# Latent attention rows in a two-layer diffusion backbone: the softmax division on GpSimd, and a fixed order of the small steps

## The chip, the cores and the metric

The kernel runs on one core of a Trainium2 chip. The metric is the device time of one execution in microseconds (us), taken as the median of repeated runs. TensorE does the matmuls and transposes, VectorE and ScalarE the elementwise work out of PSUM, GpSimd (POOL in the profile) elementwise work between SBUF tiles, and SyncE issues most of the loads.

## The reference, cut to what matters

Two layers of a diffusion backbone, on 512 latent tokens and 256 context tokens, float32 throughout. Layer 0 mixes by two head groups side by side: four heads of gated linear attention (GLA) and eight heads of softmax attention. The change lies in layer 0, where the latent queries attend to all 768 keys while the readouts of the GLA heads (second pair) are finished:

```python
def _softmax_attend(q, k, v):
    s = jnp.einsum('bhgqd,bhkd->bhgqk', q, k, preferred_element_type=jnp.float32) * (ATT_HEAD_DIM ** -0.5)
    p = jax.nn.softmax(s, axis=-1).astype(v.dtype)
    return jnp.einsum('bhgqk,bhkd->bhgqd', p, v)

def _gated_readout(o, og, gain):
    return _merge(_rms(o, gain) * jax.nn.silu(og))
```

The results of both groups stand side by side (`cat`), and one output projection follows, then the feed-forward parts and layer 1.

## The kernel before, in words

**The stage.** `Attention.latent` (L285 on) works through 32 rows, one for each of four tiles of 128 latent tokens and each of eight heads; a row is a 128x768 block of probabilities. It is a generator with 37 steps: step i makes the scores of row i, turns row j = i - 3, and in every second step multiplies two turned rows with the values. The steps of one row:

- `scores` (L178): four matmuls of TensorE into an `S` tile (tag `mm`, two buffers of two banks each); VectorE takes the row minimum (`amx`, L193; the scores carry a minus sign), ScalarE the exponential with its sum (`prob`, `asm`, L195), VectorE the reciprocal of the sum (`ars`, L196) and the division, as a multiplication by a per-partition scalar (L198).
- `turned` (L200): three steps later six transposes `pT`, the first four into a `tr` tile (two buffers), the last two into one of the two single banks `sc0` and `sc1`; then two copies back to SBUF (`probT`, L210), 128x512 and 128x256. ScalarE does both, except that VectorE takes the second one in every fourth row.
- `values` (L212): 24 matmuls into `attO`, which takes the `sc` bank of its token tile (t % 2). After the last head of a tile, `done` (L231) has ScalarE round the result to `x` (L763) and VectorE form the remainder (L764).
- `other` (L148) says which `sc` bank the transposes may use: the one that `attO` does not hold, or, once a tile is in the list `ended`, that tile's own bank. `done` puts the tile on the list at once, so that the next step's transposes go to the bank that L763 and L764 are just reading.
- `queries` (L166), after steps 4, 12 and 20: four transposes `qT` (in a `tr` tile), then ScalarE, VectorE, ScalarE, VectorE take one half each (`qs`, L174 and L175).

**The work behind it.** The table `behind` in `even_mixer` (L1270) names what follows the attention step i: `t` transposes a readout (`catT`, L1329 on) and splits it into `x` (L1330, L1331); `r1` is one readout of the second head pair (L1222 on) for two token tiles; `M` is a group of modulation columns: 64 small matmuls `mod_acc`, and later `modT`. A readout takes squares on ScalarE (`sq`, L1228), their sum on VectorE (L1230), a power on GpSimd (`rs`, L686), and two VectorE multiplications of 128x512 elements with both inputs in SBUF, by `rs` (L1233) and by the gate `og` (L1235).

**What sets the order.** TensorE's instructions keep the order in which the program is written (`pin`). On VectorE, ScalarE and GpSimd a scheduler chooses the order from the dependencies, and it may pull a step ahead of its place in the program: of the three `r1`, two run before row 0 of the latent attention, and one in the middle of the loop. The splits of weights for the output projection (`wH` on ScalarE, L803; `wL<-raw,wH` on VectorE, L804, both inputs in SBUF) are placed by the scheduler as well. A pair of existing functions fixes an order: `order_from` (L1594) remembers the last instruction written, and `order_to` makes each later instruction of an engine depend on the one written before it on that engine.

Of the kernel before, what the change touches and what calls it, by code (L numbers as in the profile page):

```python
# [8 lines left out]
F32 = mybir.dt.float32  # L9
# [3 lines left out]
AF = mybir.ActivationFunctionType  # L13
ALU = mybir.AluOpType
AX = mybir.AxisListType
PSUM = bass.MemoryType.PSUM

P = 128
# [4 lines left out]
NT = SEQ + CTX  # L23
NTT = NT // P
LT = SEQ // P
# [108 lines left out]
class Attention:  # L134
# [150 lines left out]
    def latent(self, ap):  # L285
        kl = [ap.tile([P, 2, SEQ], F32R, name=f"k{x}") for x in "HL"]
        self.k[0] = [kl] + self.k[1]
        q = lambda t: ap.tile([P, 8, P], F32R, tag="qs", bufs=2, name=f"qs{t}")
        self.keys(0, LT, kl)
        yield  # L290
        self.queries(0, q(0))
        yield

        ahead = 3
        ps, pTs, due = {}, {}, []
        for i in range(8 * LT + ahead + 2):
            t, hd = divmod(i, 8)
            if t < LT:
                ps[i] = ap.tile([P, NT], F32, tag="prob", bufs=4, name="prob")
                self.scores(t, (hd,), ps[i][:, None, :])  # L300
            j = i - ahead
            if 0 <= j < 8 * LT:
                pTs[j] = ap.tile([P, NTT, P], F32, tag="probT", bufs=4, name="probT")
                self.turned(ps.pop(j), pTs[j], (1,) if j % 4 == 3 else (), self.other())
            if due:
                t0, n, xs = due.pop()
                self.values(t0, n, xs)
                if n == 3:
                    self.done(t0)
            if 0 <= j < 8 * LT and j % 2:  # L310
                due.append((j // 8, j // 2 % 4, [pTs.pop(x) for x in (j - 1, j)]))
            if t + 1 < LT and hd == 4:
                self.queries(t + 1, q(t + 1))
            yield


class Net:
# [797 lines left out]
    def even_mixer(self, h, mix, z):  # L1115
        nc, I = self.nc, self.I
# [5 lines left out]
        tiles = (4, 0, 2)  # L1122
# [84 lines left out]
        def job(c, i):  # L1207
            t0, nt = ((LT, 2), (0, LT))[i]
            ends.setdefault(c, [])
            return self.gla_job(gp, c, t0, nt, fs[c][i], gq[c], gk[c], gv, *((ends[c], None) if i else (None, ends[c])))  # L1210
# [11 lines left out]
        def readout(c, tiles=tiles):  # L1222

            for t0 in tiles:
                cs = slice(256 * c, 256 * c + 256)
                o = gv[:, t0 : t0 + 2, cs].rearrange("p t (h v) -> p t h v", h=2)
                sq = self.wp.tile([P, WU], F32, tag="mraw", bufs=2, name="sq")[:, :512]
                nc.scalar.activation(sq.rearrange("p (t n) -> p t n", t=2), gv[:, t0 : t0 + 2, cs], AF.Square)  # L1228
                ss = self.sm.tile([P, 4], F32, tag="ss4", name="ss4")
                nc.vector.tensor_reduce(ss, sq.rearrange("p (x v) -> p x v", v=P), axis=AX.X, op=ALU.add)  # L1230
                rs = self.rstd(ss, P, 4)
                rb = rs.rearrange("p (t h) -> p t h", t=2)[:, :, :, None].to_broadcast([P, 2, 2, P])
                nc.vector.tensor_tensor(o, o, rb, op=ALU.mult)  # L1233
                x = gv[:, t0 : t0 + 2, cs]
                nc.vector.scalar_tensor_tensor(x, x, 0.5 if c else 1.0, og[c][:, t0 : t0 + 2, :], op0=ALU.mult, op1=ALU.mult)  # L1235


        kinds = {
            "q": lambda: nat(1536 + 288, ev_q), "kv": lambda: nat(1536 + 544, ev_kv), "m": lambda: mods,
            "qk0": lambda: qk(0), "qk1": lambda: qk(1), "v0": lambda: values(0), "v1": lambda: values(1),  # L1240
            "g0": lambda: gates(0), "g1": lambda: gates(1), "p": lambda: self.att_prep(mixg, natq, natk),
            "c0": lambda: job(0, 0), "l0": lambda: job(0, 1), "c1": lambda: job(1, 0), "l1": lambda: job(1, 1),
            "e": decays, "r0": lambda: (readout(0, (t,)) for t in tiles), "r1": lambda: (readout(1, (t,)) for t in tiles),
            "x": lambda: att.context(), "y": lambda: att.latent(ap),
            "t": lambda: self.gated_T(lambda t, hh: gv[:, t, hh * P : (hh + 1) * P], 4, R_GG, cat, ((4, 2), (0, 4))),
            "M": lambda: self.mod_group(0, 4, ["wL"] * 4 + ["wH"] * 3 + ["raw"]),
# [2 lines left out]
        att = Attention(self, natq, natk, cat)  # L1249
        running = {"qk0": early}  # L1250

        def run(steps):
            for x in steps.split():
                if x not in running:
                    running[x] = kinds[x]()
                next(running[x], None)
# [10 lines left out]
        with self.pool("att") as ap:  # L1267
            run("y x y g1 x y x y M x y")

            behind = {6: "t", 7: "r1", 9: "t", 10: "r1", 14: "M", 15: "r1", 16: "M", 17: "t", 19: "t", 22: "t", 24: "t", 26: "t", 29: "t"}  # L1270
            for i in range(3, 32 + 5):
                run("y " + behind.get(i, ""))
        self.pinned = False
        return cat

# [1009 lines left out]
```

## Time and profile before

| | |
|---|---|
| median of 3 runs | 1674.96 us (1674.84 to 1675.24) |
| the profiled execution | 1675.78 us, its span 1674.0 us |
| TensorE (PE) busy | 1644.8 us, 98% of the span |
| VectorE (DVE) busy | 1311.1 us, 78% |
| ScalarE (ACT) busy | 916.1 us, 55% |
| GpSimd (POOL) busy | 129.4 us, 8% |
| granted TensorE clock | 0.998 of full speed |

The span is what the profiler sees of the program; 1.8 us of the execution's time lie around it. The profiled execution is a run of its own, 0.8 us longer than the median. In the page, "L198" is line 198 of the kernel, `out<-in` are the program's names of the tiles, and "idle before" is how long the engine stood still ahead of those instructions, with the engine that ended the wait behind an arrow. A span of a group in a timeline is pipelined: the next instruction may start before the shown end of the one in front of it.

### The profile page before, as it was taken

What the parts mean: (1) busy time and instruction counts of PE and PEld (TensorE: products, weight loads), DVE (VectorE), ACT (ScalarE), POOL (GpSimd) and SP (SyncE); (2) the same over time, 40 slices, a digit from 0 to 9 for tenths busy, and PEclk for the clock granted to TensorE, in tenths of its full rate; (3) what the DMA queues carried; (4) which work ended last, traced back from release to release, by engine and by line L of the source; (5) the groups of instructions that cost most, each with busy time, mean ns of one, the idle gap of its engine ahead of it and who ended that gap; (6) DMA issues with size and microseconds to landing.
All of it is one profiled execution on the core that took longest, in us unless ns stands there. A gap on an engine that the chain in (4) does not pass through costs nothing.

```text
span 1674.0 us, 32524 instructions
## 1 busy us (share of the span) xinstructions
PE 1644.8 (98%) x13407; PEld 1481.1 (88%) x13407; DVE 1311.1 (78%) x2097; ACT 916.1 (55%) x1551; POOL 129.4 (8%) x139
## 2 busy tenths in 40 slices
PE   9999999999999999999999999999999999999998
PEld 7899987888999999998887888888888899999886
DVE  5999678976898988777668648788775599987887
ACT  5745567845544443446447436666664565555664
POOL 2004110011000000002102000000000100000310
PEclk9999999999999999999999999999999999999999
DMA  9641012164243445249525541121124333333973
GB/s 336 213 132 41 3 45 86 50 227 160 80 126 114 139 151 176 78 153 205 100 84 193 200 127 57 48 65 40 51 65 150 126 114 115 114 101 102 226 164 138
DMA packets 184736, 204.79 MB, mean 122 GB/s; under 512 B 7142, under 2 KB 141836, under 8 KB 184588
## 3 DMA queue, kind: packets, MB, share of 16 engines
q1 hardware_dynamic: 173996, 181.98, 34.7%
q0 software_dynamic: 9024, 17.30, 5.9%
q10 hardware_dynamic: 1568, 3.43, 0.6%
q8 instruction: 105, 1.72, 0.4%
q14 instruction: 43, 0.35, 0.1%
HBM read 193.23 MB, written 9.46 MB: 121 GB/s over the span
## 4 chain that ended last, share of the span: by engine, by line
PE 83%; DVE 8%; ACT 3%; DMA 3%; issue 2%; POOL 0%; SPq 0%; DVEq 0%; ACTq 0%; POOLq 0%
PE nat L355 12%; PE a L355 10%; PE ff L355 8%; PE E L355 7%; PE oproj L355 6%; PE x L355 6%; PE o L355 5%; PE D L355 4%; PE b L355 3%; PE fq L355 3%; PE gqk L355 2%; PE pearly L355 2%; PE q L355 2%; PE S L355 2%; PE poh L355 1%
## 5 line engine op out<-in xcount | busy, mean ns | idle before, releaser
L355 PE MATMUL nat<-wH,x 128*128 128x256 f32 (+2 forms) x968 | 226.7, 322 | 1.2 <-ACT x L2014 0.6
L860 ACT CAST wH<-raw 128x1024 fp32r<-128x1024 f32 x120 | 124.8, 1051 | 102.7 <-DVE raw L885 40.7
L355 PEld LDWEIGHTS nat<-wH,x 128*128 128x128 f32 x968 | 161.9, 190 | 19.5 <-ACT natq L1196 1.7
L861 DVE TENSOR_TENSOR wL<-raw,wH 128x1024 fp32r<-128x1024 f32 x120 | 145.7, 1222 | 23.6 <-ACT wH L860 23.3
L355 PE MATMUL nat<-wL,x 128*128 128x256 f32 (+2 forms) x484 | 153.5, 317 | 1.8 <-DVE wL L804 1.8
L804 DVE TENSOR_TENSOR wL<-raw,wH 128x1024 fp32r<-128x1024 f32 x79 | 95.8, 1222 | 50.6 <-ACT wH L803 49.8
L355 PE MATMUL ff<-x,wH 128*128 128x512 f32 (+1 forms) x512 | 127.6, 340 | 0.0
L686 POOL TENSOR_TENSOR rs<-ms,neghalf 128x1 f32<-128x1 f32 (+2 forms) x56 | 60.1, 1076 | 777.7 <-DVE ms L684 777.6
L803 ACT CAST wH<-raw 128x1024 fp32r<-128x1024 f32 x79 | 82.2, 1050 | 68.5 <-PE ff L355 19.7
L355 PE MATMUL oproj<-wH,x 128*128 128x512 f32 x320 | 102.2, 394 | 0.4 <-ACT x L1330 0.4
L355 PEld LDWEIGHTS nat<-wL,x 128*128 128x128 f32 x484 | 92.1, 190 | 7.8 <-DVE wL L804 2.7
L615 DVE SCALAR_TENSOR_TENSOR macc<-mraw,scT,macc 128x1024 f32<-128x1024 f32 x70 | 88.0, 1282 | 11.6 <-DMA mraw<-in_mod_w_dram 11.4
L355 PEld LDWEIGHTS ff<-x,wH 128*128 128x128 f32 x512 | 87.3, 190 | 10.0
L355 PE MATMUL x<-wH,two 128*128 128x512 f32 x280 | 90.5, 392 | 0.9 <-DVE y L1851 0.7
L1773 POOL DMA_DIRECT2D t<-in_ffn_w_down_dram x36 | 41.9, 1200 | 640.1 <-DVE t L1812 338.3
L1012 ACT COPY qkh<-arr 128x512 f32<-128x512 f32 x112 | 70.2, 641 | 36.6 <-DVE arr L1017 32.3
L355 PE MATMUL ff<-x,wL 128*128 128x256 f32 (+1 forms) x256 | 86.2, 337 | 0.0
L885 DVE TENSOR_TENSOR raw<-raw 128x512 f32<-128x512 f32 x120 | 82.8, 690 | 2.8
L1017 DVE TENSOR_TENSOR arr<-arr,f 128x512 f32<-128x512 f32 x112 | 74.4, 688 | 2.0 <-ACT qkh L1012 0.3
L355 PEld LDWEIGHTS oproj<-wH,x 128*128 128x128 f32 x320 | 59.9, 188 | 13.0 <-ACT x L1330 1.0
L355 PE MATMUL a<-T,wH 128*128 128x384 f32 (+1 forms) x320 | 70.5, 309 | 0.6 <-ACT qb L923 0.5
L355 PE MATMUL E<-T,wH 128*128 128x384 f32 (+1 forms) x320 | 70.4, 309 | 0.7 <-DVE go L938 0.7
(425 smaller groups left out, 4558.6 us busy)
## 6 DMA issues: line engine op xcount, KB each, us to landing
mraw<-in_mod_w_dram SPq DMA_DIRECT2D x80, 512.0 KB, 4.4
raw<-in_ffn_w_gate_dram SPq DMA_DIRECT2D x44, 512.0 KB, 3.9
raw<-in_ffn_w_up_dram SPq DMA_DIRECT2D x44, 512.0 KB, 4.9
raw<-in_odd_w_in_dram SPq DMA_DIRECT2D x40, 512.0 KB, 3.7
t<-in_ffn_w_down_dram POOLq DMA_DIRECT2D x30, 512.0 KB, 8.3
raw<-in_ffn_w_down_dram SPq DMA_DIRECT2D x28, 512.0 KB, 8.0
mraw<-in_mod_w_dram SPq DMA_DIRECT2D x32, 256.0 KB, 6.3
raw<-in_even_w_in_dram SPq DMA_DIRECT2D x16, 512.0 KB, 5.9
```

The source lines that it names most:

```text
L355: return self.pin(self.nc.tensor.matmul(*a, **k))
L615: nc.vector.scalar_tensor_tensor(a, u, w, a, op0=ALU.mult, op1=ALU.add)
L686: nc.gpsimd.tensor_tensor(rs, ms, self.neghalf.to_broadcast([P, w]), op=ALU.pow)
L803: self.casts = self.casts[-1:] + [nc.scalar.copy(H[:, :m], raw[:, :m])]
L804: vector.tensor_tensor(L[:, :m], raw[:, :m], H[:, :m].bitcast(F32), op=ALU.subtract)
L860: self.nc.scalar.copy(H, f)
L861: self.nc.vector.tensor_tensor(L, f, H.bitcast(F32), op=ALU.subtract)
L885: add = lambda o, x, y: nc.vector.tensor_tensor(o, x, y, op=ALU.add)
L1012: nc.scalar.copy(qkv[:, :, :, half, :], dst)
L1017: nc.vector.tensor_tensor(dst, dst, tb, op=ALU.mult)
L1773: add = lambda o, src: self.pin(nc.gpsimd.dma_start(out=o, in_=src, accum_op=ALU.add))
```

## The change

1. The division of a latent row moves from VectorE to GpSimd: a `tensor_tensor` multiplication of the 128x768 row by the reciprocal, broadcast along the row. It is written at step i for row i - 1, together with the reciprocal. The rows (`prob`) get six buffers in place of four.
2. The copies after the transposes are divided by a rule: the 128x512 one always on ScalarE, the 128x256 one always on VectorE.
3. Within a step the order is now written as: scores (TensorE); reciprocal and division of row i - 1; minimum of row i; transposes of row j; ScalarE's copy; exponential of row i; VectorE's copy; values. `order_from` and `order_to` around the loop keep ScalarE, VectorE and GpSimd to this order from step 3 on.
4. A finished tile's bank is put on the list `ended` one step later (`over`).
5. A readout of the second pair becomes a generator of four pieces (squares; sum and power; multiplication by `rs`; multiplication by `og`), and `behind` places the twelve pieces of the three readouts one by one between steps 3 and 16. The modulation group moves from steps 14 and 16 to 17 and 22, and the `t` pieces from 6 to 29 to between 8 and 28.

```diff
@@ Attention.latent
-        ps, pTs, due = {}, {}, []
+        ps, pTs, sums, due, over = {}, {}, {}, [], []
         for i in range(8 * LT + ahead + 2):
             t, hd = divmod(i, 8)
             if t < LT:
-                ps[i] = ap.tile([P, NT], F32, tag="prob", bufs=4, name="prob")
-                self.scores(t, (hd,), ps[i][:, None, :])
+                s = net.mm_tile("S")
...
+            if i - 1 in sums:
+                p, sm = ps[i - 1], sums.pop(i - 1)
+                r = net.sm.tile([P, 1], F32, tag="ars", name="ars")
+                nc.vector.reciprocal(r, sm)
+                self.scaled = nc.gpsimd.tensor_tensor(p, p, r.to_broadcast([P, NT]), op=ALU.mult)
+            if t < LT:
+                mx = net.sm.tile([P, 1], F32, tag="amx", name="amx")
+                nc.vector.tensor_reduce(mx, s[:, :NT], axis=AX.X, op=ALU.min)
             j = i - ahead
-            if 0 <= j < 8 * LT:
-                pTs[j] = ap.tile([P, NTT, P], F32, tag="probT", bufs=4, name="probT")
-                self.turned(ps.pop(j), pTs[j], (1,) if j % 4 == 3 else (), self.other())
+            turned = 0 <= j < 8 * LT
+            if turned:
...
+                for g, pt in ((0, net.tr_tile("pT")), (4, net.sc_tile("pT", self.other()))):
...
+                self.copied = nc.scalar.copy(*pts[0])
+            if t < LT:
+                ps[i] = ap.tile([P, NT], F32, tag="prob", bufs=6, name="prob")
+                sums[i] = net.sm.tile([P, 1], F32, tag="asm", name="asm")
+                nc.scalar.activation(ps[i], s[:, :NT], AF.Exp, bias=mx, scale=-1.0, accum_out=sums[i])
+            if turned:
+                self.copied = self.copied, nc.vector.tensor_copy(*pts[1])
+            self.ended += over
+            over = []
             if due:
                 t0, n, xs = due.pop()
                 self.values(t0, n, xs)
                 if n == 3:
                     self.done(t0)
+                    self.ended.remove(t0)
+                    over = [t0]
@@ even_mixer: readout(c), the loop
                 nc.scalar.activation(sq.rearrange("p (t n) -> p t n", t=2), gv[:, t0 : t0 + 2, cs], AF.Square)
+                if c:
+                    yield
...
-            behind = {6: "t", 7: "r1", 9: "t", 10: "r1", 14: "M", 15: "r1", 16: "M", 17: "t", 19: "t", 22: "t", 24: "t", 26: "t", 29: "t"}
+            behind = {
+                3: "r1", 5: "r1", 6: "r1", 7: "r1", 8: "t r1", 9: "r1", 10: "r1", 13: "r1 r1", 14: "r1", 15: "r1", 16: "r1", 17: "M",
+                18: "t", 21: "t", 22: "M", 23: "t", 24: "t", 25: "t", 26: "t", 28: "t",
+            }
+            self.order_from()
             for i in range(3, 32 + 5):
                 run("y " + behind.get(i, ""))
+            self.order_to(*att.copied, att.scaled)
```

How the instructions then stand on three engines. VectorE before, just ahead of the first latent row (`kL` and `qs` are halves of the latent keys and of the first queries; the `gvo` rows and the `ss` and `ms` rows above them are two readouts of the second pair):

```order
L1230 TENSOR_REDUCE ss_3951<-sq 128x4
L1230 TENSOR_REDUCE ss_4052<-sq 128x4
L684 TENSOR_SCALAR ms<-ss_3951 128x4
L684 TENSOR_SCALAR ms<-ss_4052 128x4
L196 RECIPROCAL rs_3569<-ss_3568 128x4
L1233 TENSOR_TENSOR gvo<-gvo,rs 128x2x256
L198 TENSOR_SCALAR prob_3557<-prob_3557,rs_3569 128x256 x4
L162 SCALAR_TENSOR_TENSOR kL<-kT,kH 64x512
L175 TENSOR_TENSOR qs_3621<-qT,qs_3621 64x512
L1235 SCALAR_TENSOR_TENSOR gvo<-gvo,og_685 128x2x256
L162 SCALAR_TENSOR_TENSOR kL<-kT,kH 64x512
```

VectorE now, at the same place:

```order
L196 RECIPROCAL rs_3569<-ss_3568 128x4
L198 TENSOR_SCALAR prob_3557<-prob_3557,rs_3569 128x256 x4
L162 SCALAR_TENSOR_TENSOR kL<-kT,kH 64x512
L175 TENSOR_TENSOR qs_3621<-qT,qs_3621 64x512
L162 SCALAR_TENSOR_TENSOR kL<-kT,kH 64x512
L175 TENSOR_TENSOR qs_3621<-qT,qs_3621 64x512
```

The eight readout instructions are gone from here; they stand in the loop.

VectorE before, around the second tile's queries (`qs`, after step 4):

```order
L193 TENSOR_REDUCE amx<-S 128x1
L196 RECIPROCAL ars<-asm 128x1
L175 TENSOR_TENSOR qs_3837<-qT,qs_3837 64x512
L198 TENSOR_SCALAR prob<-prob,ars 128x768
L196 RECIPROCAL ars<-asm 128x1
L198 TENSOR_SCALAR prob<-prob,ars 128x768
L175 TENSOR_TENSOR qs_3837<-qT,qs_3837 64x512
L193 TENSOR_REDUCE amx<-S 128x1
```

VectorE now, at the same place:

```order
L311 RECIPROCAL ars<-asm 128x1
L315 TENSOR_REDUCE amx<-S 128x1
L333 COPY probT<-pT 128x256
L175 TENSOR_TENSOR qs_3836<-qT,qs_3836 64x512 x2
L311 RECIPROCAL ars<-asm 128x1
L315 TENSOR_REDUCE amx<-S 128x1
L333 COPY probT<-pT 128x256
L1265 TENSOR_REDUCE ss_3883<-sq 128x4
L717 TENSOR_SCALAR ms<-ss_3883 128x4
L311 RECIPROCAL ars<-asm 128x1
```

The divisions (L198) are gone, both `qs` halves stand together, ahead of step 5's reciprocal and minimum, and the readout's sum stands behind step 5's copy.

ScalarE now, from step 4's exponential to step 7's (the two CASTs are the halves of the queries):

```order
L331 ACTIVATE prob,asm<-S,amx 128x768
L174 CAST qs_3836<-qT 64x512 x2
L327 COPY probT<-pT 128x512
L331 ACTIVATE prob,asm<-S,amx 128x768
L327 COPY probT<-pT 128x512
L331 ACTIVATE prob,asm<-S,amx 128x768
```

GpSimd now, from the latent keys to the end of the stage (before, only one `rs` row stood between the `kL` row and the twelve `rs` rows of 128x1):

```order
L164 CAST kL<-kL 64x512
L312 TENSOR_TENSOR prob<-prob,ars 128x768 x5
L719 TENSOR_TENSOR rs<-ms,neghalf 128x4
L312 TENSOR_TENSOR prob<-prob,ars 128x768 x4
L719 TENSOR_TENSOR rs<-ms,neghalf 128x4
L312 TENSOR_TENSOR prob<-prob,ars 128x768 x5
L719 TENSOR_TENSOR rs<-ms,neghalf 128x4
L312 TENSOR_TENSOR prob<-prob,ars 128x768 x18
L719 TENSOR_TENSOR rs<-ms,neghalf 128x1 x12
```

GpSimd has 32 divisions now, and the powers of the three readouts stand between them.

More of the change, by code (lines that the diff above doesn't have):

```diff
@@ L292, in latent @@
         yield
+        nc, net = self.nc, self.net
         ahead = 3
-        ps, pTs, due = {}, {}, []
+        ps, pTs, sums, due, over = {}, {}, {}, [], []
         for i in range(8 * LT + ahead + 2):
             t, hd = divmod(i, 8)
+            last = []
             if t < LT:
-                ps[i] = ap.tile([P, NT], F32, tag="prob", bufs=4, name="prob")
-                self.scores(t, (hd,), ps[i][:, None, :])
-            j = i - ahead
-            if 0 <= j < 8 * LT:
-                pTs[j] = ap.tile([P, NTT, P], F32, tag="probT", bufs=4, name="probT")
-                self.turned(ps.pop(j), pTs[j], (1,) if j % 4 == 3 else (), self.other())
+                s = net.mm_tile("S")
+                at = 0
+                for ks in self.k[0]:
+                    m = ks[0].shape[-1]
+                    for x, k in enumerate(ks):
+                        net.mm(s[:, at : at + m], self.q[t][:, hd, :], k[:, hd // 4, :], start=(x == 0), stop=(x == 1))
+                    at += m
+            if i - 1 in sums:
[6 more added lines that the diff above has]
+                nc.vector.tensor_reduce(mx, s[:, :NT], axis=AX.X, op=ALU.min)
+            j = i - ahead
+            turned = 0 <= j < 8 * LT
+            if turned:
+                p = ps.pop(j)
+                pTs[j] = pT = ap.tile([P, NTT, P], F32, tag="probT", bufs=4, name="probT")
+                pts = []
+                for g, pt in ((0, net.tr_tile("pT")), (4, net.sc_tile("pT", self.other()))):
+                    n = min(4, NTT - g)
+                    for x in range(n):
+                        net.tr(pt[:, x * P : (x + 1) * P], p[:, (g + x) * P : (g + x + 1) * P], net.ident)
+                    pts.append((pT[:, g : g + n, :], pt[:, : n * P].rearrange("p (c i) -> p c i", c=n)))
+                self.copied = nc.scalar.copy(*pts[0])
[7 more added lines that the diff above has]
+            over = []
@@ L309, in latent @@
                     self.done(t0)
-            if 0 <= j < 8 * LT and j % 2:
+                    self.ended.remove(t0)
+                    over = [t0]
+            if turned and j % 2:
                 due.append((j // 8, j // 2 % 4, [pTs.pop(x) for x in (j - 1, j)]))
@@ L1231, in readout @@
                 rs = self.rstd(ss, P, 4)
+                if c:
+                    yield
                 rb = rs.rearrange("p (t h) -> p t h", t=2)[:, :, :, None].to_broadcast([P, 2, 2, P])
                 nc.vector.tensor_tensor(o, o, rb, op=ALU.mult)
+                if c:
+                    yield
                 x = gv[:, t0 : t0 + 2, cs]
                 nc.vector.scalar_tensor_tensor(x, x, 0.5 if c else 1.0, og[c][:, t0 : t0 + 2, :], op0=ALU.mult, op1=ALU.mult)
+                if c:
+                    yield
         kinds = {
@@ L1242, in even_mixer @@
             "c0": lambda: job(0, 0), "l0": lambda: job(0, 1), "c1": lambda: job(1, 0), "l1": lambda: job(1, 1),
-            "e": decays, "r0": lambda: (readout(0, (t,)) for t in tiles), "r1": lambda: (readout(1, (t,)) for t in tiles),
+            "e": decays, "r0": lambda: (next(readout(0, (t,)), None) for t in tiles), "r1": lambda: readout(1),
             "x": lambda: att.context(), "y": lambda: att.latent(ap),
```

## The prediction

> **What bounds the kernel now.** I read the table of stretches first, with its cuts at the two ends of the stage. Its columns are the stretch and its length, then the busy time of PE, PEld, DVE, ACT and POOL, the granted clock, and the DMA share.
>
> ```profile
> 236.00:253.25 17.25, 14.92 (x144) 13.25 (x142) 13.94 (x28) 9.49 (x27) 4.49 (x6) 1.00 0.35 108
> 253.25:332.87 79.62, 75.71 (x746) 63.41 (x748) 69.30 (x129) 63.85 (x134) 1.28 (x1) 1.00 0.19 64
> 341.28:500.00 158.72, 158.69 (x847) 145.69 (x847) 126.81 (x149) 80.98 (x139) 10.68 (x12) 1.00 0.47 146
> ```
>
> TensorE is the bound before, in and after the stage. It is idle for 79.62 - 75.71 = 3.91 us in the loop and 2.33 us in the lead-in, and for 0.03 us in the 159 us behind it. So a microsecond of TensorE idleness that goes or comes here is a microsecond of the end. The matmuls stay the same, and so all that the change can win is 3.91 + 2.33 = 6.2 us (0.37%). A measurement of this kernel can tell about 0.2% (3.35 us) from no change.
>
> The waits of TensorE between 236 and 342 us say what these idle times wait for:
>
> ```profile
> PE pT L358 <- DVE x L764: 2.1, 3, 1.3
> PE attO L355 <- DVE probT L210: 1.4, 1, 1.4
> PE pT L358 <- DVE kL L162: 0.6, 1, 0.6
> PE pT L358 <- DVE probT L210: 0.5, 2, 0.3
> PE qT L358 <- ACT probT L210: 0.5, 1, 0.5
> PE S L355 <- ACT prob L195: 0.4, 1, 0.4
> ```
>
> The chain of waits, in order of time, gives TensorE's own pace over two steps:
>
> ```profile
> 309.99 0.90 PE S L355 x4
> 310.89 0.66 PE pT L358 x6
> 311.55 0.22 PE catT L358 x2
> 311.77 0.70 PE S L355 x4
> 312.47 0.66 PE pT L358 x6
> 313.13 1.46 PE attO L355 x24
> 314.59 0.90 PE S L355 x4
> ```
>
> A pair of steps takes 314.59 - 309.99 = 4.6 us, a short one of about 1.6 and a long one (with `attO`) of about 3.0.
>
> **Change by part.** *What goes from VectorE and ScalarE.* By group, between 250 and 342 us:
>
> ```profile
> L198 DVE TENSOR_SCALAR prob<-prob,ars 128x768 f32<-128x768 f32 x32 | 19.7, 617 | 0.6
> L210 DVE COPY probT<-pT 128x256 f32<-128x256 f32 x8 | 3.3, 414 | 3.2 <-PE pT L358 3.2
> L210 ACT COPY probT<-pT 128x256 f32<-128x256 f32 x24 | 9.2, 384 | 0.5 <-PE pT L358 0.3
> ```
>
> VectorE loses 19.7 us of divisions and gains 24 copies x 0.414 = 9.9 us; ScalarE loses 9.2 us. Neither is TensorE time: they count only through the waits.
>
> *The lead-in* loses two readouts from VectorE (eight instructions ahead of row 0). The 1.4 us wait for `probT` and the 0.6 us wait for `kL` are waits for VectorE, which stands in that queue. Worth -2.0 us, with little doubt. The readouts don't vanish; they come back in the loop, below.
>
> *The bank a step later* takes the wait of `pT` for `x` L764 away: another bank is used for one step, and L763/L764 get two steps. Together with the other waits of the loop the whole 3.91 us can go. I take all of them away and count new ones afresh.
>
> *The fixed order: one row's loop.* VectorE's minimum, ScalarE's exponential and VectorE's next reciprocal now follow each other in a ring (reciprocal i, minimum i+1, exponential i+1, reciprocal i+1). Timeline rows of VectorE, ScalarE and TensorE, and two of the chain:
>
> ```profile
> 298.89 0.95 DVE L193 TENSOR_REDUCE amx<-S 128x1 f32<-128x768 f32 x1
> ```
> ```profile
> 299.93 0.90 ACT L195 ACTIVATE prob<-S,amx 128x768 f32<-128x768 f32 x1 [0.23 <-DVE amx L193]
> ```
> ```profile
> 300.98 0.50 PE L355 MATMUL S<-kH,qs 128*128 128x512 f32 x1 [0.43 <-ACT prob L195]
> ```
> ```profile
> 278.94 1.01 ACT prob L195 x2
> ...
> 279.97 0.17 DVE ars L196
> ```
>
> Minimum to exponential 1.04, exponential to reciprocal 1.03, with 0.07 from the reciprocal to the next minimum 2.1 us a row: under TensorE's 2.3, so an undisturbed ring costs nothing, but it makes up only 0.2 us a row when it is late. An `S` bank is free 1.05 us after its exponential began (299.93 to 300.98).
>
> *The queries (steps 4, 12, 20).* Both `qs` halves stand together on both engines, and ScalarE's second half waits for VectorE's first, as rows of VectorE and ScalarE show it for `kH`/`kL`, then for `qs`:
>
> ```profile
> 245.82 0.67 DVE L162 SCALAR_TENSOR_TENSOR kL<-kT,kH 64x512 fp32r<-64x512 f32 x1
> 246.52 0.68 DVE L175 TENSOR_TENSOR qs<-qT,qs 64x512 fp32r<-64x512 f32 x1
> 247.24 1.14 DVE L1235 SCALAR_TENSOR_TENSOR gvo<-gvo,og 128x512 f32<-128x512 f32 x1
> ...
> 250.59 0.69 DVE L1235 SCALAR_TENSOR_TENSOR gvo<-gvo,og 128x512 f32<-128x512 f32 x1
> ```
> ```profile
> 246.53 0.59 ACT L161 ACTIVATE kH<-kT 64x512 fp32r<-64x512 f32 x1 [2.86 <-DVE kL L162]
> 247.24 0.58 ACT L174 CAST qs<-qT 64x512 fp32r<-64x512 f32 x1
> ```
>
> With T as the start of step 4's scores: scores to 0.90, minimum from 0.92, exponential 1.96 to 2.85, ScalarE's half to 3.44, VectorE's to 4.14, the second halves to 4.77 and 5.48. Step 5's minimum is queued behind them: it starts at 5.5 though its scores were ready at 2.7. Its exponential starts at 6.54, its bank is free at 7.6. TensorE wants that bank for step 7 at 0.90 + 0.66 + 0.44 (`qT`, as two `catT` for two) + 0.70 + 0.66 + 1.46 + 0.90 + 0.66 = 6.4. So it waits 1.2 us, at three places: +3.6. If the ring enters such a place late by d, the wait is 1.2 + d; I take d = 0.5: +1.5 more, with 0 and 1.5 a place as ends. The cover that would hide this is another matmul group between the scores of steps 5 and 7; there is none (`mod_acc` stands behind step 17).
>
> *GpSimd's division.* No row shows it at 128x768. The nearest:
>
> ```profile
> L1382 POOL TENSOR_TENSOR natq<-natq,rs 128x512 f32<-128x512 f32 x6 | 7.0, 1180 | 15.1 <-DVE natq L1381 14.8
> L1382 POOL TENSOR_TENSOR natk<-natk,rs 128x128 f32<-128x128 f32 x6 | 3.5, 598 | 2.2 <-DVE glaf L1018 2.2
> L686 POOL TENSOR_TENSOR rs<-ms,neghalf 128x4 f32<-128x4 f32 x14 | 17.3, 1237 | 376.9 <-DVE ms L684 376.9
> ```
>
> Per element (1180 - 598) / 384 = 1.52 ns; 598 + 640 x 1.52 = 1.57 us. The ends: 1.2 (no longer than 512) and 1.18 x 768/512 = 1.8, to 2.6 if the broadcast costs double. I take 1.57, from the same operation with a broadcast `rs`. [...] At 1.57 it is hidden: by the ring's times row i's division ends some 4.8 us after its scores begin (0.92 + 1.04 + 1.03 + 0.2 + 1.57), and its transposes come three steps and 0.90 later, 7.1 us or more.
>
> *The shared way to SBUF.* In the VectorE rows above, the same `gvo` multiplication takes 1.14 us once and 0.69 once. GpSimd's rows beside it:
>
> ```profile
> 246.56 0.61 POOL L164 CAST kL<-kL 64x512 fp32r<-64x512 f32 x1 [1.07 <-DVE kL L162]
> 247.22 0.61 POOL L164 CAST kH<-kH 64x512 fp32r<-64x512 f32 x1
> ```
>
> The slow one starts with GpSimd's cast at 247.22 and ends 0.55 after the cast's end: it stood still. `qs` at 246.52, with one input in PSUM, kept its 0.68 beside a cast. [...] This speaks against the change: its divisions hold that way for 1.57 of 2.3 us. They begin 0.2 after the reciprocal and end 1.77 after; VectorE reaches an added instruction after minimum and copy, 1.3 after. The three multiplications by `og` wait 0.5 and end at 2.4: 0.3 beyond the ring. The three by `rs` are released by a power on GpSimd (1.24), behind which the next division starts at once: they wait out all of it, 1.3 beyond the ring. Three `wL` (1.2 us each, steps 17 to 19) end at about 3.0: 0.9 beyond. Lateness 0.9 + 3.9 + 2.7 = 7.5 us. An undisturbed exponential frees its bank 3.0 us after its scores begin, and TensorE wants it after 4.6: 1.6 us of slack, more than any one of these costs, so only what meets another reaches TensorE. I take a third: +2.4, with 0 and 5 as ends.
>
> *Sum.* -2.0 - 3.9 + 3.6 + 1.5 + 2.4 = +1.6 us against the profiled 1675.78: 1677.4. The median stands 0.8 lower, so 1674.96 + 1.6 = 1676.6. `M` and `t` move with their matmuls, and GpSimd's other work starts only after the stage: nothing.
>
> **The rivals.**
>
> *The waits really go (faster).* For it: VectorE has 69.3 of 79.6 us to do in the loop now, and less than that afterwards. It needs the query halves not to hold up the next minimum and the divisions not to hold up VectorE. Against it: queue and waits above. All but about 0.8 us of 6.2 gone: -5.4, 1669.6.
>
> *Only the queries cost.* The shared way is too seldom in conflict to reach TensorE: -5.9 + 3.6 = -2.3, 1672.7.
>
> *Lateness adds up (slower).* The divisions' hold and the query halves meet: the last `wL` and L764 stand on VectorE just ahead of step 20's queries. It decides where the ring enters a query step over 1 us late. Then query places cost 2.2 each and the rest 4.3: -5.9 + 6.6 + 4.3 = +5, 1680.
>
> *GpSimd becomes the bound (slower).* At 2.6 us a division, 32 x 2.6 + 3 x 1.24 = 86.9 us against the loop's 79.6: +7.3 - 2.0 = +5.3, 1680.3. It decides from about 2.3 us on.
>
> **How the numbers follow.** Forecast 0.42 (between -1 and +3.3, nearly always); waits go 0.12; only the queries 0.18; lateness adds up 0.22; GpSimd the bound 0.06. Faster by over 0.2%: 0.13 (the first rival and a remnant). Within: 0.18 + most of the forecast = 0.53. Slower: 0.22 + 0.06 + 0.06 = 0.34. The range takes in all but the first rival and little above: 1671.0 to 1681.0.
>
> **What would show it.** Right: the lead-in's idle time near 0.4; new TensorE waits two to three steps behind each query, `S` for the exponential or `pT` for the 128x256 copy; `gvo` and `wL` of over 1 us on VectorE where they lie beside divisions; divisions of 1.5 to 1.8 us. Wrong: a loop in which TensorE idles under 2 us (faster), waits of `pT` for GpSimd throughout (GpSimd the bound), or idle time that arises behind 341 us.

## The result, and the profile after

The changed kernel took 1686.27 us (median of 4 runs, 1685.68 to 1686.96) against 1674.93 for the kernel before on the same chip: a ratio of 1.0068, 95% interval 1.0055 to 1.0081, so 11.3 us slower. The forecast was +1.6 and the range ended at 1681.0. The profiled execution has a span of 1683.9 us; it ends 9.9 us later than the one of before.

The table of stretches of the changed kernel, cut at the same place in the lead-in and at the end of the stage's last `attO` (columns as in the prediction):

```profile
236.00:253.25 17.25, 16.67 (x161) 15.02 (x160) 10.93 (x22) 10.08 (x27) 2.46 (x4) 1.00 0.37 115
253.25:352.94 99.69, 87.78 (x823) 69.99 (x822) 69.07 (x134) 61.27 (x119) 49.82 (x35) 0.98 0.19 66
352.94:500.00 147.06, 146.55 (x777) 133.66 (x778) 115.56 (x135) 75.21 (x131) 11.29 (x12) 1.00 0.47 147
```

The stage ends at 352.94 instead of 341.28, 11.7 us later; behind it 1.8 us come back (1683.9 - 352.94 = 1331.0 us against 1674.0 - 341.28 = 1332.7), so the loss lies in this stage. The lead-in got what was forecast, 0.58 us of idle TensorE instead of 2.33. The loop and its tail idle 99.69 - 87.78 = 11.9 us. The waits of TensorE between 236 and 353 us (total, times, longest):

```profile
PE catT L391 <- ACT probT L327: 2.9, 3, 1.7
PE pT L391 <- DVE probT L333: 2.3, 3, 0.9
PE attO L388 <- DVE probT L333: 1.8, 3, 0.7
PE S L388 <- ACT prob L331: 1.2, 4, 0.3
PE pT L391 <- ACT probT L327: 1.2, 2, 0.8
PE modT L391 <- ACT probT L327: 1.2, 1, 1.2
...
PE pT L391 <- POOL prob L312: 0.3, 1, 0.3
```

No wait for `x` L797 is left, so the bank that is free a step later did its work. GpSimd is waited for 0.3 us. Nearly all the rest is for copies of `probT` and exponentials that came late. What made those late stands in VectorE's groups between 240 and 356 us (total and mean of one, then the idle time ahead of them and what ended it):

```profile
L175 DVE TENSOR_TENSOR qs<-qT,qs 64x512 fp32r<-64x512 f32 x8 | 5.5, 689 | 5.8 <-ACT qs L174 5.7
L1270 DVE TENSOR_TENSOR gvo<-gvo,rs 128x512 f32<-128x512 f32 x3 | 5.2, 1732 | 0.0
L797 DVE TENSOR_TENSOR x<-attO,x 128x512 fp32r<-128x512 f32 x6 | 4.1, 688 | 6.9 <-ACT x L796 6.9
L1376 DVE SCALAR_TENSOR_TENSOR x<-catT,col,x 128x512 fp32r<-128x512 f32 x4 | 3.0, 748 | 4.2 <-ACT x L1375 4.2
L1274 DVE SCALAR_TENSOR_TENSOR gvo<-gvo,og 128x512 f32<-128x512 f32 x3 | 2.7, 913 | 0.0
L1376 DVE SCALAR_TENSOR_TENSOR x<-catT,col,x 128x256 fp32r<-128x256 f32 x4 | 1.9, 484 | 4.7 <-ACT x L1375 4.7
```

Three kinds of instruction have the same shape: ScalarE writes the high half of a number, and VectorE subtracts it to get the low half. They are the queries (L174, L175), the finished tile (L796, L797) and `catT` (L1375, L1376). VectorE stands still ahead of them for 5.8 + 6.9 + 4.2 + 4.7 = 21.6 us; 17.2 of these lie between 253.25 and 352.94 (the finished tiles have only 2.6 there). What is queued behind it in the loop is the next row's reciprocal and minimum. One row in a step with `catT`, first on VectorE and then on ScalarE:

```profile
326.44 0.48 DVE L1376 SCALAR_TENSOR_TENSOR x<-catT,col,x 128x256 fp32r<-128x256 f32 x1 [1.18 <-ACT x L1375]
326.84 0.15 DVE L311 RECIPROCAL ars<-asm 128x1 f32<-128x1 f32 x1
326.91 0.94 DVE L315 TENSOR_REDUCE amx<-S 128x1 f32<-128x768 f32 x1
327.77 0.41 DVE L333 COPY probT<-pT 128x256 f32<-128x256 f32 x1
329.57 0.75 DVE L1376 SCALAR_TENSOR_TENSOR x<-catT,col,x 128x512 fp32r<-128x512 f32 x1 [1.39 <-ACT x L1375]
330.24 0.15 DVE L311 RECIPROCAL ars<-asm 128x1 f32<-128x1 f32 x1
330.31 0.94 DVE L315 TENSOR_REDUCE amx<-S 128x1 f32<-128x768 f32 x1
```
```profile
327.97 0.90 ACT L331 ACTIVATE prob<-S,amx 128x768 f32<-128x768 f32 x1 [1.08 <-DVE amx L315]
328.77 0.18 ACT L331 ACTIVATION_READ_ACCUMULATOR prob<-S,amx 128x1 f32 x1
328.86 0.68 ACT L1375 ACTIVATE x<-catT,col 128x512 fp32r<-128x512 f32 x1
```

From one minimum to the next it is 330.31 - 326.91 = 3.40 us. The minimum and the way to the exponential take 1.06, the exponential 0.89, then ScalarE's half 0.71, VectorE's half 0.67, and the reciprocal 0.07. The sum that the reciprocal needs is read by 328.95, but VectorE's order has the half of `catT` first, which starts at 329.57, and the reciprocal only runs at 330.24. The pair has become part of the row's ring (the chain that leads from one row's minimum to the next), which so grows from 2.1 to 3.4 us, beyond the 2.3 that TensorE needs for a step on average. (The row before it, with the half of 256 columns, takes 2.91.)

### The profile page after: what moved, and what is told of

Same layout as the page of the kernel before. It is cut to its first block, busy times and chain, and to the rows that moved or that the text cites. A ratio compares the mean times of both kernels' runs of the same rounds, so it can differ in the third digit from the quotient of the medians.

```text
span 1683.9 us, 32604 instructions
## 1 busy us (share of the span) xinstructions
PE 1648.9 (98%) x13407; PEld 1482.3 (88%) x13407; DVE 1304.3 (77%) x2089; ACT 909.0 (54%) x1527; POOL 176.0 (10%) x171
## 4 chain that ended last, share of the span: by engine, by line
PE 80%; DVE 10%; ACT 4%; DMA 4%; issue 2%; POOL 0%; DVEq 0%; SPq 0%; ACTq 0%; POOLq 0%
PE nat L388 13%; PE a L388 10%; PE ff L388 8%; PE E L388 7%; PE x L388 6%; PE oproj L388 6%; PE o L388 4%; PE b L388 3%; PE D L388 3%; PE fq L388 3%; PE gqk L388 2%; PE pearly L388 2%; PE q L388 2%; PE poh L388 1%; PE S L388 1%
## 5 line engine op out<-in xcount | busy, mean ns | idle before, releaser
L388 PEld LDWEIGHTS oproj<-wH,x 128*128 128x128 f32 x320 | 59.8, 188 | 12.6 <-ACT x L1375 0.6
L388 PE MATMUL E<-x,wH 128*128 128x384 f32 (+1 forms) x320 | 70.7, 310 | 0.0
```

Of the source, the lines that this page charges most:

```text
L388: return self.pin(self.nc.tensor.matmul(*a, **k))
```

## The experiments

Theory: the laid-out order puts three kinds of split pair into the row's ring. Rival: GpSimd's division and its hold on the way to SBUF cost the time, whatever the order. Times below are given as differences to the kernel before run on the same chip (its medians lie between 1674.25 and 1674.73), with the ratio and its interval; the changed kernel stands at +11.3.

**The scheduler's order again.**

```diff
-            self.order_from()
             for i in range(3, 32 + 5):
...
-            self.order_to(*att.copied, att.scaled)
```

> The changed kernel with all its parts, but without the two lines that lay out the order by hand: the scheduler orders the rows again. Theory of the ring: the loss comes from the laid-out order, in which VectorE's half of each split pair (queries, the finished tile's copy, the copy of catT) stands ahead of the next reciprocal and waits for ScalarE's half. Then most of the 11 us goes: 1674 to 1678. Theory of GpSimd: the division on GpSimd and its hold on the way to SBUF cost it, whatever the order: 1682 to 1686.

Measured 1671.90 us, -2.4 (0.9986, 0.9977 to 0.9996). The loss is gone with the two lines, by more than the ring's 1674 to 1678, and the divisions on GpSimd are still there. So the laid-out order costs 11.3 + 2.4 = 13.7 us, and the division on GpSimd isn't slow whatever the order: the rival falls here as the cause of the loss.

**The division back on VectorE, in the laid-out order.**

```diff
-                self.scaled = nc.gpsimd.tensor_tensor(p, p, r.to_broadcast([P, NT]), op=ALU.mult)
...
+            if i - 1 in ps and i <= 8 * LT:
+                nc.vector.tensor_scalar(p, p, r, None, op0=ALU.mult)
```

> The changed kernel with the division back on VectorE right behind the row's minimum, everything else in the laid-out order. Theory of the ring: the pairs still stand in VectorE's order ahead of the next reciprocal, and a division of some 0.5 us comes on top in VectorE: 1684 to 1690, as slow as the changed kernel or slower. Theory of GpSimd: with the division goes the lengthening of the folds and readouts: 1678 to 1682.

Measured 1686.89 us, +12.6 (1.0076, 1.0061 to 1.0091). What lengthened the readouts' multiplications beside GpSimd's divisions went away, as the same group in this kernel shows:

```profile
L1271 DVE TENSOR_TENSOR gvo<-gvo,rs 128x512 f32<-128x512 f32 x3 | 2.0, 680 | 0.0
```

0.68 us instead of 1.73, and the time did not fall. This run can't price the hold by itself, because with the division VectorE gets 0.61 us a row of its own ahead of the copy of `probT`. TensorE's waits for that copy grow from 2.3 us in three places to this:

```profile
PE pT L392 <- DVE probT L334: 8.2, 12, 1.5
```

The run shows that taking the division off GpSimd doesn't bring the time back.

**VectorE's halves one step later, ScalarE's unchanged.** The core of the edit, for one of the three kinds:

```diff
-                nc.vector.scalar_tensor_tensor(L, pt, gain, H.bitcast(F32), op0=ALU.mult, op1=ALU.subtract)
+                def rest(L=L, pt=pt, H=H):
+                    nc.vector.scalar_tensor_tensor(L, pt, gain, H.bitcast(F32), op0=ALU.mult, op1=ALU.subtract)
...
+                    self.postponed.append(rest)
...
+            for f in net.postponed:
+                f()
```

The last loop stands in `latent` right behind the next row's minimum.

> The changed kernel with VectorE's half of each split pair (queries, the finished tile's copy, the copy of catT) written one step later, right behind the next row's minimum; ScalarE's halves stay. Theory of the ring: VectorE no longer stands waiting for ScalarE ahead of the reciprocal, the row-to-row time of the reduces in the steps with catT falls from 3.0 to 3.4 us to at most 2.5 us, and the time falls by at least 8 us, to 1671 to 1677. Theory of GpSimd: at most 2 us below the changed kernel, 1684 to 1686.

Measured 1675.79 us, +1.5 (1.0010, 1.0000 to 1.0019): 9.8 of the 11.3 us come back. In VectorE's rows of this kernel, at the same kind of step, the half no longer waits, and VectorE stands ready for the reciprocal 0.2 to 0.5 us ahead of time; behind them the row of ScalarE's exponential between:

```profile
318.54 0.96 DVE L329 TENSOR_REDUCE amx<-S 128x1 f32<-128x768 f32 x1
...
320.71 0.16 DVE L325 RECIPROCAL ars<-asm 128x1 f32<-128x1 f32 x1 [0.48 <-ACT prob L348]
321.94 0.96 DVE L329 TENSOR_REDUCE amx<-S 128x1 f32<-128x768 f32 x1 [1.07 <-PE S L405]
322.81 0.74 DVE L1394 SCALAR_TENSOR_TENSOR x<-catT,col,x 128x512 fp32r<-128x512 f32 x1
323.47 0.41 DVE L350 COPY probT<-pT 128x256 f32<-128x256 f32 x1
324.10 0.16 DVE L325 RECIPROCAL ars<-asm 128x1 f32<-128x1 f32 x1 [0.22 <-ACT prob L348]
324.25 0.96 DVE L329 TENSOR_REDUCE amx<-S 128x1 f32<-128x768 f32 x1
```
```profile
323.01 0.90 ACT L348 ACTIVATE prob<-S,amx 128x768 f32<-128x768 f32 x1
```

From 321.94 to 324.25 is 2.31 us. The row before it still takes 3.40 (318.54 to 321.94), so the expected 2.5 us at most did not come out for it: its minimum waited 1.07 for its scores, so here TensorE sets the pace, with its long step and the `catT`. Two rows together take 5.71 us in place of 2.91 + 3.40 = 6.31. The hold of GpSimd's division is as large here (1.84 us) as in the changed kernel (1.73):

```profile
L1287 DVE TENSOR_TENSOR gvo<-gvo,rs 128x512 f32<-128x512 f32 x3 | 5.5, 1836 | 0.0
```

What it costs, this run doesn't tell.

**One kind of pair at a time.** The same edit for the queries alone, for `catT` alone, and for the finished tile alone.

> The changed kernel with VectorE's half of the queries alone (three places, two instructions each) one step later; the pairs of catT and of the finished tile stand as laid out. Theory that the queries are most of it (the step of the prediction that had 3.6 us there, too small): 1676 to 1679. Theory that catT's and the finished tile's pairs, which the prediction had at nothing, are half or more of it: 1680 to 1683.

> The changed kernel with VectorE's half of catT alone one step later; queries and finished tiles as laid out. Theory that the queries are most of it: 1683 to 1686. Theory that catT's pairs are half or more of it: 1678 to 1682, and the row-to-row time of the reduces in the steps with catT falls to about TensorE's 2.3 to 2.5 us.

> The changed kernel with VectorE's half of the finished tile's copy alone (three places) one step later; queries and catT as laid out. If the three kinds of pair add up: 10.5 - 4.9 - 4.3 = 1.3 us below the changed kernel, about 1685. If the finished tile alone brings nothing and the kinds help each other: 1686 to 1687. If it is as large as the others: 1681 to 1683.

Measured: queries 1681.33, +6.6 (1.0041, 1.0027 to 1.0056); `catT` 1682.00, +7.3 (1.0044, 1.0029 to 1.0059); finished tile 1682.94, +8.5 (1.0050, 1.0037 to 1.0062). They give back 4.7, 4.0 and 2.8 us, together 11.5 where all at once give 9.8. Taken one by one, each interval still touches that of the changed kernel (1.0055 to 1.0081), so the three sizes are estimates. Shown is that together they make nearly all of the loss against the kernel before (9.8 of 11.3), though not all that the laid-out order costs against the scheduler's: 1675.79 is still 3.9 us above 1671.90. That the queries alone are most of it (1676 to 1679) did not come out.

**One engine's order at a time.**

```diff
-            self.order_to(*att.copied, att.scaled)
+            self.order_to(att.copied[0], att.scaled)
```

This lays out ScalarE's order and, with `att.scaled`, GpSimd's too; the text on record for this run below has GpSimd's order as the scheduler's, which the edit doesn't do. The other run lays out VectorE's order alone:

```diff
-            self.order_to(*att.copied, att.scaled)
+            self.order_to(att.copied[1])
```

> The changed kernel with ScalarE's order alone laid out by hand; VectorE's and GpSimd's are the scheduler's. Theory that VectorE's order does the harm (its half of a pair stands in front of a reciprocal that is ready): most of the 11 us goes, 1673 to 1678. Rival, that ScalarE's order does it (its half of a pair stands behind an exponential that isn't ready): 1682 to 1687.

> The changed kernel with VectorE's order alone laid out by hand; ScalarE's and GpSimd's are the scheduler's. Theory that VectorE's order does the harm: 1680 to 1686. Rival, that ScalarE's order does it: 1673 to 1678, since ScalarE's halves then come ahead of the exponentials.

Measured: ScalarE's with GpSimd's 1680.90, +6.2 (1.0039, 1.0024 to 1.0054); VectorE's alone 1679.55, +4.8 (1.0028, 1.0019 to 1.0037). Neither theory holds as stated: each of the two gives back about half. A pair has a half on each engine, and I read it so that either order puts it into the ring; that reading isn't shown. The two runs differ in GpSimd's order as well, and ScalarE's run is not clean for a second reason: the scheduler put a readout in front of a minimum on VectorE there. Rows of VectorE and GpSimd:

```profile
276.02 1.95 DVE L1270 TENSOR_TENSOR gvo<-gvo,rs 128x512 f32<-128x512 f32 x1 [1.05 <-POOL rs L719]
277.90 0.94 DVE L315 TENSOR_REDUCE amx<-S 128x1 f32<-128x768 f32 x1
```
```profile
274.99 1.01 POOL L719 TENSOR_TENSOR rs<-ms,neghalf 128x4 f32<-128x4 f32 x1
275.96 1.47 POOL L312 TENSOR_TENSOR prob<-prob,ars 128x768 f32<-128x768 f32 x1
```

The readout waited 1.05 us for the power, which takes 1.01, and then ran for 1.95 us with all of the next division beside it. TensorE idled 2.7 us for the copy of `probT` behind the minimum (the stretch from 276 us in the last section). That is the rival's mechanism at one place, in an order of VectorE that the changed kernel doesn't have. With the slow clock behind it (by estimate 1.6 us, last section), it is some 4 of the 8.6 us between this kernel and the scheduler's order, so how the loss divides between the two engines' orders stays open.

**What the division is worth.** The division back on VectorE in the scheduler's order, and in the order with the halves a step later; and the division on GpSimd as the only part of the change in the kernel before (the `tensor_scalar` of a row replaced by the `tensor_tensor` on GpSimd, with six buffers for the rows in place of four).

> The changed kernel in the scheduler's order (no order laid out) with the division back on VectorE: what is left of the change is the finished bank a step later, the readouts in pieces and the other places of readouts and catT. If the division on GpSimd is what brings the scheduler's version below the kernel before: 1674 to 1676, as before. If pieces and places bring it: 1671 to 1673, as the scheduler's version with the division on GpSimd (1671.9).

> The laid-out order with VectorE's halves a step later (1675.8), and the division back on VectorE. With the pairs out of the way, the disputed hold of GpSimd's division on folds and readouts stands alone. If it costs TensorE what the prediction had (2.4 us): 1672 to 1674. If it costs nothing, and VectorE's own 0.45 us a row does: 1677 to 1683. Neither: 1675 to 1677.

> The kernel before with one edit: the row's division runs on GpSimd, in the scheduler's own order. Theory of the ring: near the kernel before, 1672 to 1676, since no order is laid out. Theory of GpSimd: several us slower than before, about 1680.

Measured: 1675.35, +0.8 (1.0002, 0.9993 to 1.0011); 1678.45, +3.9 (1.0024, 1.0015 to 1.0033); 1674.86, +0.6 (1.0002, 0.9992 to 1.0012). Without GpSimd the scheduler's order loses 3.2 us and the postponed one 2.4, though in both cases the ends of the two intervals just overlap; alone in the kernel before the move brings nothing. So the division on GpSimd is probably a gain where it meets the rest of the change, and in none of these a loss that can be told from none.

**What else makes the scheduler's version faster.** Readouts in one piece again; the finished bank free at once; and the bank a step later added to the kernel before with the division on GpSimd.

```diff
-                    self.ended.remove(t0)
-                    over = [t0]
```

> The changed kernel in the scheduler's order with each readout in one piece again, at steps 7, 10 and 15 as before. If the pieces bring the scheduler's version below the kernel before: 1674 to 1676. If they don't: 1671 to 1673.

> The changed kernel in the scheduler's order with the finished bank free at once, as before. If the bank a step later is what brings the scheduler's version below the kernel before: 1674 to 1676. If the places of the groups bring it: 1671 to 1673.

> The kernel before with the division on GpSimd and the finished bank free a step later, in the scheduler's order with the places of before. If the bank brings the gain: 1671 to 1673. If the places bring it: 1674 to 1676, as the division alone (1674.9).

Measured: 1672.43, -2.1 (0.9986, 0.9977 to 0.9994); 1675.82, +1.4 (1.0006, 0.9997 to 1.0015); 1672.99, -1.5 (0.9989, 0.9980 to 0.9998). The four pieces bring nothing; the bank does: the intervals of the scheduler's version with it and without it don't meet (0.9977 to 0.9996 against 0.9997 to 1.0015). The wait for `x` in the kernel with the division alone, in the one with division and bank, and in the scheduler's version without the bank:

```profile
PE pT L361 <- DVE x L767: 1.8, 3, 1.3
```
```profile
PE pT L365 <- DVE x L771: 0.3, 1, 0.3
```
```profile
PE pT L389 <- DVE x L795: 2.6, 3, 1.3
```

In the scheduler's version with the bank one such wait of 1.1 us is left. Without the bank TensorE also waits 1.4 us for a division of GpSimd, so the wait for `x` is not the whole difference between the two.

**A candidate.** Laid out with postponed halves up to step 8 alone (the call of `order_to` under `if i == 8:`), the scheduler's from there.

> A candidate to beat both: the laid-out order with VectorE's halves a step later up to step 8 alone, which keeps the lead-in free of readouts, and the scheduler's order from there. Theory of the ring, with both gains together: 1669 to 1672. If the scheduler moves readouts into the lead-in all the same, or the first eight steps lose what the lead-in wins: 1672 to 1676.

Measured 1674.22, -0.3 (0.9996, 0.9987 to 1.0005): no gain over the scheduler's order throughout. Its lead-in keeps the gain (16.67 us busy of 17.25, against 15.03 in the scheduler's order), but up to 343 us its loop idles 5.6 us against 2.8. The best version is the change without its laid-out order, 0.14% under the kernel before: less than the 0.2% that the prediction named as telling, though the interval excludes no change.

## Why the prediction was wrong

The forecast of +1.6 missed the measured +11.3 by 9.7 us. By these runs two steps of the prediction made that up, in about equal parts.

- **"`M` and `t` move with their matmuls: nothing": the first step that failed.** A matmul group brings its copies, and each `t` brings ScalarE and VectorE halves into the fixed order. The prediction had worked out just this pattern for the queries and did not look for it elsewhere. `catT` alone gave back 4.0 us and the finished tile, which it did not count as a pair at all, 2.8; both were priced at zero. All three kinds together gave back 9.8, where the prediction had 5.1 for the queries alone: 4.7 of the 9.7.
- **"the whole 3.91 us can go. I take all of them away and count new ones afresh": the second.** The count of the new ones stopped too early. Without the queries the prediction's terms add up to -2.0 - 3.9 + 2.4 = -3.5; the kernel with VectorE's halves a step later, in which the pairs no longer hold up the ring, measured +1.5 (0.0 to +3.2). That is the other 5.0 us. Its laid-out order still leaves 89.75 - 83.85 = 5.9 us of idle TensorE behind the lead-in:

```profile
253.25:343.00 89.75, 83.85 (x821) 68.25 (x821) 69.80 (x134) 62.21 (x121) 49.79 (x35) 1.00 0.21 73
```

The six waits for the 128x256 copy (2.5 us) and three for the 128x512 one (1.3) are new ones in it. That the copies' place behind other work in a fixed order makes them is argued from the rows, not tried, and the hold below may have a part in it; the cause of this half stays open.

- **Queries, +3.6 and +1.5: the size was about right, the wait only in part.** 4.7 us came back when VectorE's halves went a step later, though that is an estimate and part of it is shared with the other pairs. The prediction had TensorE wait for the `S` bank, 1.2 us and more at each place. Behind the loop's first queries it waits 1.6 us in all, but only 0.32 for `S`; most goes to the two copies of `probT`, which stand behind the halves and the late minimum:

```profile
264.07 0.63 PE L391 MATMUL pT<-ident,prob 128*128 128x128 f32 x4 [0.37 <-ACT probT L327]
265.61 0.44 PE L391 MATMUL pT<-ident,prob 128*128 128x128 f32 x2 [0.91 <-DVE probT L333]
266.36 0.50 PE L388 MATMUL S<-kH,qs 128*128 128x512 f32 x1 [0.32 <-ACT prob L331]
```

- **"An undisturbed ring costs nothing", 2.1 us a row: nearly right.** The postponed kernel's row has 1.07 to the exponential, 1.09 to the reciprocal, and at least 0.07 from there: 2.23, still under TensorE's 2.3, with hardly a reserve. And it was disturbed in far more steps than three.
- **The shared way, +2.4: the hold was there, its price stays open.** `gvo` times `rs` took 1.73 us and `gvo` times `og` 0.91, against 0.68 each without the division: held by 1.05 and 0.23, somewhat less than the 1.57 and 0.5 worked out. Rows of VectorE and GpSimd in the changed kernel:

```profile
267.68 1.75 DVE L1270 TENSOR_TENSOR gvo<-gvo,rs 128x512 f32<-128x512 f32 x1
...
269.42 0.93 DVE L315 TENSOR_REDUCE amx<-S 128x1 f32<-128x768 f32 x1
...
270.61 1.05 DVE L1274 SCALAR_TENSOR_TENSOR gvo<-gvo,og 128x512 f32<-128x512 f32 x1
```
```profile
267.41 1.47 POOL L312 TENSOR_TENSOR prob<-prob,ars 128x768 f32<-128x768 f32 x1
269.64 1.47 POOL L312 TENSOR_TENSOR prob<-prob,ars 128x768 f32<-128x768 f32 x1 [0.76 <-DVE ars L311]
```

Both multiplications end 0.55 us after the division beside them; the minimum, which reads `S`, took 0.93 beside a division, against 0.95 in the kernel before. That a shared way to SBUF makes this was read out of such rows; the runs show the times alone. Whether TensorE stands behind it is another matter. In the changed kernel the chain of waits, followed back from the end of the stage, runs through two of the three multiplications by `rs`:

```profile
267.76 1.66 DVE gvo L1270
...
278.06 1.64 DVE gvo L1270
```

So the hold makes rows late there. The division back on VectorE takes it away but adds 0.61 us a row to VectorE's work, and that exchange brings nothing in this order and costs 2.4 us in the postponed one. No run shows the +2.4: none has the hold away and nothing else changed.
- **GpSimd's division, 1.57 us: 1.47 measured, and hidden but for one wait of 0.3 us:**

```profile
L312 POOL TENSOR_TENSOR prob<-prob,ars 128x768 f32<-128x768 f32 x32 | 46.9, 1468 | 50.9 <-DVE ars L311 39.4 <-PE pT L391 5.6 <-DMA raw<-in_even_w_out_dram 2.1
```

- **Lead-in, -2.0: right** (2.33 to 0.58). **Bank: right**, the wait for `x` is gone in the changed kernel.
- **The rival "lateness adds up"** had the sign and the kind, but of the pairs only the queries, and so 6 us too little.

Of the 11.7 us by which the stage ends later, idle TensorE is 12.49 - 6.27 = 6.2 (0.58 + 11.91, against 2.33 + 3.94 of before up to 341.28). The other 5.4 are a longer busy time. The slow clock below accounts, by estimate, for 1.6 of it. Three more matmuls of the output projection (`oproj`) stand ahead of the cut than before, eight against five; at the 0.23 us that each takes in a row they are 0.7 us of it and of the 1.8 that come back behind the stage. The remaining 3.1 stay open.

## What to carry to other kernels

Before an order is fixed by hand, list every instruction that would stand between a row's last ScalarE result and the VectorE instruction that starts the next row, those of moved matmul groups' copies too. Wherever VectorE's half waits for ScalarE's half, try the second engine's half behind the instruction that the ring needs next, not ahead of it: here that gave back 9.8 us. A step that "only moves" can have a price for each copy that it brings along. And measure the scheduler's order beside the one laid out by hand: here it was 3.9 us faster than the best laid-out one.

## What the runs showed of the hardware

Inside this stage the granted clock fell to about half for some 3.3 us in three of these profiles (the changed kernel, 0.52 over 290.00:293.30; the one with the division back on VectorE, 0.53 over the same stretch; the one with ScalarE's and GpSimd's order laid out, 0.54 over 279.20:282.50). By estimate, from the 0.52, that cost 3.3 x 0.48 = 1.6 us of TensorE's work in the changed kernel, and about as much in the other two. The changed kernel, ahead of the drop and in it, then the kernel with `catT` alone postponed over the same stretches:

```profile
286.50:290.00 3.50, 1.42 (x9) 0.80 (x8) 3.14 (x7) 2.08 (x5) 1.47 (x1) 0.96 0.00 0
290.00:293.30 3.30, 3.30 (x18) 2.78 (x20) 3.19 (x8) 2.41 (x6) 2.67 (x3) 0.52 0.00 0
...
311.50:315.00 3.50, 1.53 (x24) 1.29 (x24) 1.58 (x4) 2.54 (x5) 0.86 (x1) 1.00 0.35 128
```
```profile
286.50:290.00 3.50, 1.42 (x10) 0.78 (x8) 3.01 (x6) 2.08 (x5) 1.47 (x1) 1.00 0.00 0
290.00:293.30 3.30, 3.25 (x35) 2.59 (x35) 3.18 (x8) 2.36 (x5) 2.54 (x3) 1.00 0.00 0
```

TensorE was busy 1.42 of 3.5 us in both, and only the first lost its clock; another stretch of the first, 1.53 of 3.5, lost none. The kernel with ScalarE's and GpSimd's order laid out lost it after the clearest gap:

```profile
276.00:279.20 3.20, 0.57 (x6) 0.33 (x4) 3.17 (x4) 0.24 (x1) 1.43 (x1) 0.94 0.00 0
279.20:282.50 3.30, 3.27 (x27) 2.76 (x27) 3.18 (x5) 2.12 (x5) 1.47 (x1) 0.54 0.02 5
```

TensorE had just waited 2.7 us there, and the drop behind it costs some 1.6 by the estimate above. What sets off a drop isn't shown: 1.42 busy of 3.5 us stood ahead of one in one kernel and of none in the other.
